# Input operators of an S5 mixer built with channel and position on the partitions: transposes in the mixer against more work in the preparation

## The chip, the cores and the metric

The kernel runs on one core of a Trainium2 chip. The core has a matrix engine (TensorE, PE in the profile; its weight loads are PEld), a vector engine (VectorE, DVE), a scalar engine (ScalarE, ACT), a general engine (GpSimd, POOL) and a sync engine (SyncE, SP), which here issues nearly all DMAs. Each engine works off its own queue in order. The metric is the device time of one execution in microseconds; lower is better.

## What is computed

The reference is a trunk of two layers over 512 positions of 1024 channels. Each layer is a half-step feed-forward block (FFN), a token mixer and a second FFN; layer 0 mixes by pooling, layer 1 by a bidirectional S5 state space. Only the S5 input side matters here:

```python
def s5_mixer(h, lam_re, lam_im, log_dt, b_re, b_im, c_re, c_im, d_skip, w_glu, b_glu):
    u = hf.reshape(Bsz, S, SSM_GROUPS, SSM_GROUP_DIM)          # 64 groups of 16 channels
    for direction in range(N_DIRS):
        ar, ai, bb_re, bb_im = zoh_discretise(lam_re[direction], ..., b_im[direction])
        bu_re = jnp.einsum('bsgh,gph->bsgp', u, bb_re)         # 64 states per group
        bu_im = jnp.einsum('bsgh,gph->bsgp', u, bb_im)
        xr, xi = complex_linear_scan(ar, ai, bu_re, bu_im, reverse=(direction == 1))
        y = y + einsum(xr, c_re) - einsum(xi, c_im)
    ...
```

## The kernel before

**Chunks.** The S5 mixer cuts the 512 positions into 64 chunks of L = 8. For a group, one matrix takes the 8 x 16 = 128 inputs of a chunk (position j, channel h) to the 64 complex states at the chunk's end. This matrix is a power of the transition times B, so its entries are products of a table over (state, j) and the given B over (state, h). There are 64 groups, two directions, real and imaginary part. They are called w1 here; w2 (states to outputs), w3 (inputs to outputs within a chunk) and rt (rotations for the scan) are its companions. All are made on the chip beforehand, written to DRAM (w1d, w2d, w3d, rd) and loaded again in the mixer, one batch b of eight groups at a time.

**Three stages of preparation** run in the background of the FFNs, as Python generators in a queue, `bgq`. Each call of `self.prep()` (L476) runs one to its next `yield`. `S5Prep.tables` (L132) makes the powers `pw` and the input table `gp` on DVE, in the first FFN of layer 0. `S5Prep.blocks` (L272) multiplies tables with B and C on POOL, in the second FFN of layer 0: 32 steps, one for each half batch hb and direction d. `products` (L283) makes E (for w2), bt and F (for w1) in ten POOL instructions, all from the helper `mul` (L277). `matrices` (L317) does 16 small matmuls (L326) on bt and E of both directions, evacuates them on ACT and DVE into kt, and stores E, F and kt. `S5Prep.rotation` (L212) makes rt on DVE in the first FFN of layer 1.

**Where the calls lie.** In an FFN, PE does 48 matmuls for each tile m of the hidden layer (two weights q) and calls `prep` after the first 24; in the output phase it is called after every second d. Weights come as `raw` by SP, are split by ACT and DVE into `whi`, `wlo` (L651, L652; `W.adv` prepares one and issues one DMA), and three matmuls (L658 to L660) stand for one product. Whatever is left in `bgq` is drained at hooks in the last output phase of an FFN: `spare` in layer 0, `operators` in layer 1.

**The transposes.** F lies with state on the partitions and (h, j) along the free axis. The mixer needs (j, h) on the partitions. `s5_flip` (L1093) therefore turns the loaded w1 of a batch on PE: 16 transposes of 128x128 (L1099) into four PSUM banks, and four ACT copies (L1100) back into w1. It is called eight times: w1[0] in a hook of the FFN before the mixer (L1638), w1[1] at its start, the others one or two batches ahead of use.

**The mixer's loop** (L1334). For a batch, `s5_state` (L1108) does 64 matmuls (L1119), then a chain on DVE: turn by rt (L1128), scan (L1141), turn back into X (L1128, L1150). `s5_out` does 16 matmuls with w3 (L1179) and 128 with X (L1187), ACT copies yj (L1192), `s5_turn` does 32 small ones (L1202). `s5_norm` (L1285, L1287, L1290) prepares the inputs u. From b = 2, `glu_mm` adds six matmuls of the gated layer behind the mixer.

## Time and profile before

| | |
|---|---|
| median of 3 runs (lowest to highest) | 1744.36 us (1743.97 to 1745.93) |
| the profiled execution's own time | 1743.41 us |
| its span, first to last instruction | 1741.5 us |
| mean granted TensorE clock | 0.984 of full |
| share of the span of DVE and POOL on the chain that ended last | 6% and 5% (PE 80%) |
| DMA packets | 126821, 290.62 MB |

The span is what the trace shows; 1.9 us of the execution lie around it. An engine's busy share says how much it works, not what the end waits for: for that one reads who made PE wait, and where. Matmuls are pipelined, so that one record (0.39 us for 512 columns) is longer than the distance to the next (0.23 us); costs on PE are taken from starts.

### The profile page before, as it was taken

Reading aid. Unit: us, or ns where it says so; the run is one execution under the profiler, and the core shown is the slowest. Engines: PE = TensorE matmul, PEld = TensorE weight load, DVE = VectorE, ACT = ScalarE, POOL = GpSimd, SP = SyncE. Lnnn points to the kernel's source line nnn. Section 1 sums busy time; section 2 is a strip of 40 time slices with the busy share of each in tenths; the row PEclk is TensorE's granted clock in tenths of the full one; section 3 lists DMA queues with packets and bytes.
Section 4 is the critical chain, followed back from the end, with each engine's and each line's share of the span. In section 5 each row is a group of like instructions: output and inputs, shape, how many; then the busy total and the mean of one; then the engine's idle time right before and its main releaser. Section 6 shows DMA issues by size and latency. Waiting matters only on the chain.

```text
span 1741.5 us, 25135 instructions
## 1 busy us (share of the span) xinstructions
PE 1686.2 (97%) x9872; PEld 1408.9 (81%) x9872; DVE 1135.3 (65%) x1845; ACT 573.8 (33%) x875; POOL 406.5 (23%) x370
## 2 busy tenths in 40 slices
PE   8999999998999999998999999987999999999997
PEld 6887888888887887887888888877888988888886
DVE  7768878678777667666766567647868654333435
ACT  5321322354321322233332233245633532222322
POOL 0000000056699999993000000001000000000000
PEclk9999999998999999998999999999999999999999
DMA  9357567441568777664443454487645253223321
GB/s 381 126 163 263 174 195 242 131 142 31 169 199 272 211 211 257 190 190 130 136 138 106 133 155 157 144 272 250 232 169 197 96 169 109 97 92 100 109 77 58
DMA packets 126821, 290.62 MB, mean 167 GB/s; under 512 B 19904, under 2 KB 57152, under 8 KB 125680
## 3 DMA queue, kind: packets, MB, share of 16 engines
q1 hardware_dynamic: 126080, 288.31, 51.0%
q8 instruction: 77, 1.26, 0.3%
q10 hardware_dynamic: 544, 0.52, 0.1%
q0 software_dynamic: 80, 0.20, 0.1%
q14 instruction: 40, 0.33, 0.1%
HBM read 261.85 MB, written 31.33 MB: 168 GB/s over the span
## 4 chain that ended last, share of the span: by engine, by line
PE 80%; DVE 6%; POOL 5%; DMA 4%; issue 2%; ACT 1%; SPq 1%; DVEq 0%; POOLq 0%; ACTq 0%
PE ps L658 24%; PE ps L659 24%; PE ps L660 24%; POOL e L277 3%; PE ps L605 2%; PE ps L1187 2%; DMA mw<-modw 2%; POOL E L277 1%; DVE tmp L713 1%; DMA raw<-win 1%; POOL F L277 1%; DVE hlo L716 1%; DVE mw L609 1%; POOL bt L277 1%; DVE wlo L652 1%
## 5 line engine op out<-in xcount | busy, mean ns | idle before, releaser
L658 PE MATMUL ps<-hlo,whi 128*128 128x512 f32 (+3 forms) x1488 | 566.0, 380 | 7.0 <-DVE hlo L716 6.9
L659 PE MATMUL ps<-hhi,whi 128*128 128x512 f32 (+3 forms) x1488 | 562.0, 378 | 0.0
L660 PE MATMUL ps<-hhi,wlo 128*128 128x512 f32 (+3 forms) x1488 | 561.6, 377 | 0.3 <-DVE wlo L652 0.3
L652 DVE TENSOR_TENSOR wlo<-raw,whi 128x1024 fp32r<-128x1024 f32 (+2 forms) x260 | 335.7, 1293 | 111.1 <-ACT whi L651 106.8
L651 ACT CAST whi<-raw 128x1024 fp32r<-128x1024 f32 (+2 forms) x273 | 274.2, 1010 | 374.4 <-PE ps L659 196.3
L658 PEld LDWEIGHTS ps<-hlo,whi 128*128 128x128 f32 x1488 | 280.8, 189 | 62.7 <-DVE hlo L716 6.5
L660 PEld LDWEIGHTS ps<-hhi,wlo 128*128 128x128 f32 x1488 | 281.1, 189 | 52.6 <-DVE wlo L652 0.8
L659 PEld LDWEIGHTS ps<-hhi,whi 128*128 128x128 f32 x1488 | 281.2, 189 | 50.5
L658 PE MATMUL ps<-glo,whi 128*128 128x512 f32 (+1 forms) x738 | 278.6, 378 | 0.0
L659 PE MATMUL ps<-ghi,whi 128*128 128x512 f32 (+1 forms) x738 | 278.0, 377 | 0.0
L660 PE MATMUL ps<-ghi,wlo 128*128 128x512 f32 (+1 forms) x738 | 278.0, 377 | 0.0
L609 DVE SCALAR_TENSOR_TENSOR mw<-mw,condb 128x1024 f32<-128x1024 f32 x144 | 198.5, 1385 | 21.2 <-DMA mw<-modw 20.8
L651 ACT CAST ghi<-tmp 128x512 fp32r<-128x512 f32 x96 | 59.6, 620 | 401.5 <-DVE tmp L727 395.4
L727 DVE TENSOR_TENSOR tmp<-ps,tmp 128x512 f32<-128x512 f32 x88 | 60.7, 690 | 171.0 <-PE ps L660 150.4
L658 PEld LDWEIGHTS ps<-glo,whi 128*128 128x128 f32 x738 | 140.3, 190 | 28.4 <-issue 0.6
L660 PEld LDWEIGHTS ps<-ghi,wlo 128*128 128x128 f32 x738 | 139.9, 190 | 27.7
L659 PEld LDWEIGHTS ps<-ghi,whi 128*128 128x128 f32 x738 | 140.0, 190 | 27.3
L732 DVE SCALAR_TENSOR_TENSOR x<-ps,m,x 128x512 f32<-128x512 f32 (+1 forms) x107 | 74.2, 694 | 111.2 <-PE ps L660 111.2
L652 DVE TENSOR_TENSOR glo<-tmp,ghi 128x512 fp32r<-128x512 f32 x96 | 74.8, 780 | 60.5 <-ACT ghi L651 60.4
L277 POOL TENSOR_TENSOR e<-T,pr 128x576 f32<-128x576 f32 x64 | 104.8, 1657 | 21.6 <-DMA pr<-s5bc 19.7
L970 POOL TENSOR_SCALAR x<-x,pbs 128x512 f32<-128x512 f32 (+1 forms) x10 | 15.3, 1535 | 362.4 <-ACT tmp L676 361.7
L1468 POOL TENSOR_TENSOR hhi<-hlo,rstd 128x256 f32<-128x256 f32 x3 | 2.7, 911 | 371.5 <-DVE rstd L697 371.5
(285 smaller groups left out, 1597.5 us busy)
## 6 DMA issues: line engine op xcount, KB each, us to landing
raw<-win SPq DMA_DIRECT2D x162, 512.0 KB, 3.6
mw<-modw SPq DMA_DIRECT2D x144, 512.0 KB, 4.7
raw<-wout SPq DMA_DIRECT2D x32, 512.0 KB, 3.6
raw<-wout SPq DMA_DIRECT2D x32, 448.0 KB, 3.3
raw<-wout SPq DMA_DIRECT2D x32, 384.0 KB, 3.1
w2d<-E SPq DMA_DIRECT2D x64, 128.0 KB, 4.6
w1d<-F SPq DMA_DIRECT2D x32, 256.0 KB, 4.2
w<-w1d SPq DMA_DIRECT2D x8, 1024.0 KB, 8.0
```

The costliest lines, as they stand in the source:

```text
L277: nc.gpsimd.tensor_tensor(out=o, in0=x, in1=y, op=op)
L605: nc.tensor.matmul(ps[m][q], lhsT=lhs[:, k], rhs=rhs, start=i == 3 * KD, stop=i == 1)
L609: self.nc.vector.scalar_tensor_tensor(out=w, in0=w, scalar=1.0, in1=self.condb, op0=ALU.mult, op1=ALU.mult, accum_out=dst)
L651: self.nc.scalar.copy(out=hi, in_=src)
L652: (eng or self.nc.vector).tensor_tensor(out=lo, in0=src, in1=hi.bitcast(F32), op=ALU.subtract)
L658: mm(ps, lhsT=hi[:, k], rhs=rhs[1][:, cs], start=start, stop=False)
L659: mm(ps, lhsT=hi[:, k], rhs=rhs[0][:, cs], start=False, stop=False)
L660: mm(ps, lhsT=lo[:, k], rhs=rhs[0][:, cs], start=False, stop=stop)
L713: nc.vector.scalar_tensor_tensor(out=t, in0=self.x[d][:, cs], scalar=A[:, d:d + 1], in1=r, op0=ALU.mult, op1=ALU.mult)
L727: nc.vector.tensor_tensor(out=t[0:n, cs], in0=pu[:, cs], in1=t[0:n, cs], op=ALU.mult)
L732: self.nc.vector.scalar_tensor_tensor(out=self.x[d][:, cs], in0=ps[:, cs], scalar=scale[:, d:d + 1], in1=self.x[d][:, cs], op0=ALU.mult, o ...
L1187: nc.tensor.matmul(o(HB * h + g + e), lhsT=X[d][k][r, ri, g + e], rhs=w2[r, d, g + e, ri ^ k], start=False, stop=d + k + ri + g // 2 == 4)
```

## The change

w1 is now made directly with (channel h, position j) on the 128 partitions, as [part, group, state] along the free axis. `tables` turns `gp` on PE (eight matmuls against a 64x64 identity for each direction), copies it on ACT into `tu`, and writes it with 16 small DMAs to a DRAM table `ud`; the DVE copies U1 and U2 are gone. In `blocks`, `params` issues two more DMAs for each step, each spreading 2 KB rows over partitions (`ud` over the 16 channels, the given B, as a new input `s5bt`, over the 8 positions; 256 KB each). F is made from these: two products of 128x512, then a difference and a sum of 128x256 each, in place of two products and one sum of 128x512. `s5_flip` and its eight calls go.

The order changes too. E and F of a step are stored two steps later (`store`), `matrices` of hb runs a step later (bt has 4 buffers), a last step stores the rest, and an FFN's tail calls `prep` once more if it is the layer's second. In layer 1 `early` loads w1, w2 and w3 of batch 0 ahead of the rotation instead of behind it.

```diff
@@ tables
+            ps = psum.tile([P, 8, 64], F32, name="ps")
+            for ri in range(2):
+                for kb in range(4):
+                    nc.tensor.matmul(ps[:, 4 * ri + (kb if d else 3 - kb)], lhsT=gp[0:64, ri, 2 * kb:2 * kb + 2],
+                                     rhs=ident[0:64, 0:64], start=True, stop=True)
+            tu = pool.tile([P, 2, 4, 64], F32, name="tu")
+            nc.scalar.copy(out=tu.rearrange("p r k n -> p (r k) n"), in_=ps)
+            for k2 in range(2):
+                for ri in range(2):
+                    for k in range(4):
+                        nc.sync.dma_start(out=self.ud[d, 2 * k + (k2 if d else 1 - k2), :, ri],
+                                          in_=tu[64 * k2:64 * k2 + 64, ri, k])
+            yield
-            v.tensor_copy(out=o(self.U1), in_=gp[:, 0, js])
-            v.tensor_scalar(out=o(self.U2), in0=gp[:, 1, js], scalar1=self.sgn, scalar2=-1.0,
-                            op0=ALU.mult, op1=ALU.mult)
@@ blocks: params
+            ub = pool.tile([P, 2, 2, HB * 64], F32, name="ub", bufs=2)
+            for i, t in enumerate((self.ud[d, :, hb].rearrange("j r g n -> j (r g n)").unsqueeze(0),
+                                   I["s5bt"][d, hb].unsqueeze(1))):
+                nc.sync.dma_start(out=ub[:, i].rearrange("p r x -> p (r x)"),
+                                  in_=t.to_broadcast([16, L, 2 * HB * 64]))
@@ blocks: products
-            sf = [P, HB, 16, 8]
+            sf = [P, 2, HB * 64]
-            ub = lambda t: t[:, d, gs].unsqueeze(2).to_broadcast(sf)
-            bb = lambda k: pr[:, k].unsqueeze(3).to_broadcast(sf)
-            mul(f1, ub(self.U1), bb(2))
-            mul(f2, ub(self.U2), bb(3))
-            mul(Ft, f1, f2, ALU.add)
+            mul(f1, ub[:, 0, 0:1].to_broadcast(sf), ub[:, 1])
+            mul(f2, ub[:, 0, 1:2].to_broadcast(sf), ub[:, 1])
+            mul(Ft[:, 0], f1[:, 0], f2[:, 1], ALU.subtract)
+            mul(Ft[:, 1], f1[:, 1], f2[:, 0], ALU.add)
@@ blocks: the loop
-            if before:
-                matrices(*before)
-            made = [products(hb, 0)]
-            yield
-            shifts()
-            made.append(products(hb, 1))
-            before = hb, made
-            yield
+            made = []
+            for d in range(2):
+                if len(stores) > 1:
+                    store(*stores.pop(0))
+                if d and before:
+                    matrices(*before)
+                made.append(products(hb, d))
+                stores.append((hb, d, *made[d][1:]))
+                if d:
+                    before = hb, made
+                yield
+                if d == 0:
+                    shifts()
+        for o in stores:
+            store(*o)
+        yield
@@ ffn, tail
+                if f:
+                    self.prep()
@@ s5_state
-                                         lhsT=w1[:, 2 * h + d, g, 64 * ri:64 * ri + 64], rhs=ut[:, h * HB + g],
+                                         lhsT=w1[:, 2 * h + d, ri, g], rhs=ut[:, h * HB + g],
@@ s5_mixer, three calls, and one in the FFN before it
-        self.s5_flip(w1[1])
-            self.s5_flip(w1[b + 2])
-                    self.s5_flip(w1[b + 4])
-                                before=[operators, lambda: self.s5_flip(ops0[0][0])] + [
-                                    load(i) for i in (2, 3)])
+                                before=[operators, lambda: None] + [load(i) for i in (2, 3)])
@@ early
+                    for i in (0, 1, 3):
+                        ops0[i][0] = loads[i](pre, 0)
+                        yield
                     yield from self.prep3()
-                    for i, f in enumerate(loads):
-                        yield
-                        ops0[i][0] = f(pre, 0)
+                    yield
+                    ops0[2][0] = loads[2](pre, 0)
```

## Rows read from the trace of the kernel before

**Rows 1.** Busy time, share of the span and instructions of each engine, from the page.

```profile
PE 1686.2 (97%) x9872; PEld 1408.9 (81%) x9872; DVE 1135.3 (65%) x1845; ACT 573.8 (33%) x875; POOL 406.5 (23%) x370
```

**Rows 2.** What PE waited for, whole span: line waited for, us in total, times, longest.

```profile
PE ps L326 <- POOL bt L277: 10.0, 3, 5.8
...
PE ps L1099 <- DMA w<-w1d: 5.1, 1, 5.1
```

**Rows 3.** PE in order of time around the first turn of w1: start us, us, line, operation, count, and in brackets the idle time before it with what ended it.

```profile
1138.69 0.39 PE L841 MATMUL ps<-ghi,tws 128*128 128x512 f32 x1
...
1143.44 0.56 PE L1227 MATMUL ps<-m,ident 128*16 128x8 f32 x16
1149.13 3.67 PE L1099 MATMUL ps<-ident,w 128*128 128x128 f32 x16 [5.13 <-DMA w<-w1d]
1152.46 0.78 PE L841 MATMUL ps<-ghi,tws 128*128 128x512 f32 x1
```

**Rows 4.** PE in order of time in the mixer.

```profile
1186.99 3.34 PE L1099 MATMUL ps<-ident,w 128*128 128x128 f32 x16
...
1217.25 1.98 PE L1179 MATMUL ps<-w,hhi 128*64 128x128 f32 x16 [6.26 <-ACT yj L1192]
...
1226.86 1.97 PE L1099 MATMUL ps<-ident,w 128*128 128x128 f32 x16
...
1279.05 0.50 PE L658 MATMUL ps<-hlo,whi 128*128 128x512 f32 x1
...
1288.50 3.72 PE L1187 MATMUL ps<-w,X 64*64 64x128 f32 x128
```

**Rows 5.** DVE in order of time in the mixer; L1287 ends the inputs of batch 0, each L1128 with tmp<-ps,rt starts the chain of a batch (b = 0, 3, 6, 7 here), the last L1150 ends that of batch 7.

```profile
1188.97 0.69 DVE L1287 TENSOR_TENSOR hhi<-hhi,shift 128x512 f32<-128x512 f32 x1
...
1191.68 1.89 DVE L1128 TENSOR_TENSOR tmp<-ps,rt 128x512 f32<-128x512 f32 x3 [0.69 <-PE ps L1119]
1193.48 3.68 DVE L1128 TENSOR_TENSOR z<-tmp 128x256 f32<-128x256 f32 x2
...
1219.93 1.24 DVE L1141 TENSOR_TENSOR_SCAN ws<-d,z 128x519 f32<-128x519 f32 x1 [2.32 <-ACT d L1125]
...
1228.26 0.69 DVE L652 TENSOR_TENSOR hlo<-tmp,hhi 128x512 fp32r<-128x512 f32 x1 [2.28 <-ACT hhi L651]
...
1229.47 1.88 DVE L1128 TENSOR_TENSOR tmp<-ps,rt 128x512 f32<-128x512 f32 x3
...
1263.17 1.88 DVE L1128 TENSOR_TENSOR tmp<-ps,rt 128x512 f32<-128x512 f32 x3
...
1272.79 1.88 DVE L1128 TENSOR_TENSOR tmp<-ps,rt 128x512 f32<-128x512 f32 x3
...
1281.47 0.42 DVE L1150 SCALAR_TENSOR_TENSOR X<-ws,rt 128x256 f32<-128x256 f32 x1
```

**Rows 6.** Busy time (and instructions) of PE, PEld, DVE, ACT and POOL in the stretch in which `blocks` runs evenly, then granted clock, DMA share and GB/s.

```profile
452.50:680.00 227.50, 223.32 (x1096) 178.93 (x1097) 164.63 (x161) 60.04 (x89) 220.59 (x198) 1.00 0.74 230
```

**Rows 7.** Line 277, all POOL instructions of `products`: count, duration in ns as min/median/max, first and last start.

```profile
L277 POOL TENSOR_TENSOR e<-U,pr x64: 1062/1072/2055, 425.1 to 792.4; 128x512 f32<-128x512 f32 x64
L277 POOL TENSOR_TENSOR E<-e,e x32: 1422/1442/2300, 422.3 to 787.8; 128x576 f32<-128x576 f32 x32
...
L277 POOL TENSOR_TENSOR bt<-bt,b x32: 319/324/1199, 424.8 to 791.1; 128x64 f32<-128x64 f32 x32
L277 POOL TENSOR_TENSOR F<-e,e x32: 1282/1486/2242, 427.5 to 793.6; 128x512 f32<-128x512 f32 x32
```

**Rows 8.** POOL on line 652, both inputs full: count, min/median/max ns.

```profile
L652 POOL TENSOR_TENSOR wlo<-raw,whi x13: 1845/2395/2647, 372.3 to 1360.0; 128x1024 fp32r<-128x1024 f32 x12, 128x768 fp32r<-128x768 f32 x1
```

**Rows 9.** Groups of POOL instructions: busy us, mean ns | idle before us, releaser.

```profile
L277 POOL TENSOR_TENSOR e<-T,pr 128x576 f32<-128x576 f32 x64 | 104.8, 1657 | 21.6 <-DMA pr<-s5bc 19.7
L277 POOL TENSOR_TENSOR e<-U,pr 128x512 f32<-128x512 f32 x64 | 82.4, 1307 | 0.0
...
L277 POOL TENSOR_TENSOR F<-e,e 128x512 f32<-128x512 f32 x32 | 51.8, 1618 | 2.5
```

**Rows 10.** DVE and POOL in order of time, one meeting of the two.

```profile
496.10 2.31 DVE L609 SCALAR_TENSOR_TENSOR mw<-mw,condb 128x1024 f32<-128x1024 f32 x1
...
497.40 3.16 POOL L277 TENSOR_TENSOR e<-T,pr 128x576 f32<-128x576 f32 x2
```

**Rows 11.** POOL at the start of steps 3 and 32 of `blocks`, and PE at its small matmuls, in order of time.

```profile
452.46 2.76 POOL L277 TENSOR_TENSOR e<-T,pr 128x576 f32<-128x576 f32 x2 [14.23 <-DMA pr<-s5bc]
...
679.96 0.44 PE L326 MATMUL ps<-E,bt 128*32 128x128 f32 x4 [3.90 <-POOL bt L277]
...
784.87 2.88 POOL L277 TENSOR_TENSOR e<-T,pr 128x576 f32<-128x576 f32 x2
785.24 0.42 PE L326 MATMUL ps<-E,bt 128*32 128x128 f32 x8
...
791.49 0.66 PE L326 MATMUL ps<-E,bt 128*32 128x128 f32 x8 [5.83 <-POOL bt L277]
```

**Rows 12.** PE at the start of tile m = 8 of the first FFN, and DVE in `tables`, direction 0: the last instruction on the table gp (in the step of m = 11), and the first of the step after it (m = 12), in order of time.

```profile
157.06 0.39 PE L658 MATMUL ps<-hlo,whi 128*128 128x512 f32 x1
...
201.97 0.69 DVE L130 TENSOR_TENSOR gp<-ct,cu 128x512 f32<-128x512 f32 x1
...
208.33 1.28 DVE L202 TENSOR_SCALAR T<-pw,sgn 128x576 f32<-128x576 f32 x1
```

More of the change, by code (lines that the diff above doesn't have):

```diff
@@ L80, in alloc_keep @@
         self.T2 = keep.tile([P, 2, NG, 9], F32, name="T2")
-        self.U1 = keep.tile([P, 2, NG, 8], F32, name="U1")
-        self.U2 = keep.tile([P, 2, NG, 8], F32, name="U2")
         self.f1 = keep.tile([P, 2, NG], F32, name="f1")
@@ L130, in cmul, with tables @@
             v.tensor_tensor(out=o, in0=t, in1=u, op=op)
-    def tables(self, pool):
+    def tables(self, pool, psum, ident):
         nc, I = self.nc, self.I
@@ L197, in tables @@
             yield
+            ps = psum.tile([P, 8, 64], F32, name="ps")
[11 more added lines that the diff above has]
+            yield
             ks = slice(None) if d == 0 else slice(None, None, -1)
-            js = slice(None, None, -1) if d == 0 else slice(None)
             o = lambda t: t[:, d].rearrange("p g k -> p k g")
@@ L333, in matrices @@
             nc.vector.tensor_tensor(out=kt[:, 7], in0=kv[1][:, 7], in1=kt[:, 7], op=ALU.add)
-            for d, (_, E, Ft) in enumerate(parts):
-                ws = slice(1, 9) if d == 0 else slice(0, 8)
-                for ri in range(2):
-                    nc.sync.dma_start(out=self.w2d[b, hh, :, d, :, ri].rearrange("p g (k h) -> p g k h", h=16),
-                                      in_=E[64 * ri:64 * ri + 64, :, ws])
-                nc.sync.dma_start(out=self.w1d[b, 2 * hh + d], in_=Ft.rearrange("p g h j -> p (g h j)"))
             nc.sync.dma_start(out=self.kbd[gs].rearrange("q h k -> (q h) k"), in_=kt.rearrange("p k h -> p (k h)"))
@@ L342, in matrices, with store @@
                 self.late = b
+        def store(hb, d, E, Ft):
+            b, hh = divmod(hb, GB // HB)
+            ws = slice(1, 9) if d == 0 else slice(0, 8)
+            for ri in range(2):
+                nc.sync.dma_start(out=self.w2d[b, hh, :, d, :, ri].rearrange("p g (k h) -> p g k h", h=16),
+                                  in_=E[64 * ri:64 * ri + 64, :, ws])
+            nc.sync.dma_start(out=self.w1d[b, 2 * hh + d], in_=Ft.rearrange("p r n -> p (r n)"))
         def shifts():
@@ L355, in blocks @@
         before = self.late = None
+        stores = []
         self.pr = {}
@@ L1091, in s5_spare @@
         self.W.issue()
-    def s5_flip(self, w1):
-        nc = self.nc
-        for i in range(4):
-            ps = self.psum.tile([P, HB, P], F32, name="ps")
-            for g in range(HB):
-                nc.tensor.transpose(ps[:, g], w1[:, i, g], self.ident)
-            nc.scalar.copy(out=w1[:, i], in_=ps)
     def s5_rt(self, pool, b):
@@ L1483, in prep1 @@
         with tc.tile_pool(name="tab", bufs=1) as p:
-            yield from S.tables(p)
+            yield from S.tables(p, self.psum, self.ident)
     def prep3(self):
@@ L1724, in host_arrays @@
     k = np.stack([np.concatenate(t, 0) for t in ((cr, ci), (ci, cr), (br, bi), (bi, br))], 0)
+    bt = np.stack([A(t)[0] for t in (ssm_b_re, ssm_b_im)], 0)
+    a["s5bt"] = bt.reshape(2, 2, NG // HB, HB, 64, 16).transpose(1, 2, 5, 0, 3, 4).reshape(2, NG // HB, 16, 2 * HB * 64)
     a["s5bc"] = k.reshape(4, P, 2, NG // HB, HB, 16).transpose(1, 2, 3, 0, 4, 5)
```

19 lines of the change are left out of this document (10 added, 9 removed).

## Prediction

> **What bounds the kernel now.** I read the busy shares first. PE works 97% of the span [rows 1], so time comes back in two ways only: PE gets less to do, or one of its few waits goes. Second, the list of PE's waits. Two of them touch this change: 10.0 us on POOL's bt, in front of the small matmuls of `matrices`, and 5.1 us on the load of w1[0] [rows 2]. Third, the order of time on PE around the transposes [rows 3, 4], and on DVE in the mixer [rows 5], because there PE is not always the bound. Fourth, POOL in the preparation: between 452.5 and 680 it is busy for 220.6 of 227.5 us [rows 6]. So `blocks` runs at POOL's pace, and it ends the stage: PE stands 5.8 us at the last small matmuls until step 32 has made its bt [rows 11]. The change takes work from PE in the mixer and gives POOL more in the stage where POOL is full. The sum is the difference of two costs of like size.
>
> **The first turn of w1.** PE is free at 1144.0 (1143.44 and 0.56), waits for the load of w1[0], turns it in 3.67 us and starts the next product at 1152.46 [rows 3]. Without transposes that product starts at 1144.0, and the load comes 30 steps of background work earlier. Gain 8.5 us. What could stand in its place: `early` now runs the rotation three steps later, so some 18 DVE instructions of about 0.4 us, 7.8 us in all (an estimate from the 0.69 us of a 512-element product [rows 12], scaled to 256 elements), fall into the hook `operators` together with the stores of rd and the load of rt[0]. Three prepared weights, each 20 matmuls or 4.7 us on PE (1138.69 to 1143.44 [rows 3]), cover that; if they did not, a few us of the 8.5 are lost.
>
> **The other seven turns.** Two bounds. Upwards: the turns' own PE time, 3.34 us for w1[1] and 1.97 for each of six [rows 4], 15.2, and the 6.26 us for which `s5_out` of batch 1 waits on yj [rows 4]; the four PSUM banks of a turn are what fills the eight there, so that wait should go. Together 21. Downwards: what the DVE chain gives back. The u of batch 0 is ready at 1189.7 while the first chain starts at 1191.68 [rows 5], so the turn of w1[1] hides behind the norm. From there DVE works without a break but for 2.32 us on ACT's d0 copies [rows 5], which wait behind `s5_norm`, not behind the turns; that wait stays. A chain without a norm takes 9.62 us when nothing holds it (batch 6 to 7), one with a norm 0.69 more, 10.3 [rows 5]. Ahead of batch 3 DVE stands 2.28 us for ACT [rows 5], which goes, as ACT no longer copies w1 and PE no longer waits at 1217; then batch 3 starts at 1227.2 for 1229.47, batch 6 (10.3, 10.3 and 9.7 later) at 1257.5 and batch 7 at 1267.1 against 1272.79: 5.7 us. After the chains PE is the bound: before, X[7] is there at 1281.9 and PE takes it at 1288.50 only [rows 4, 5], as it is late by its turns. After, PE ends batch 6 at about 1268.5, does the turn of y (1.0), 36 product matmuls (8.4, 1279.05 to the L1179 before 1288.50) and 1.0 of L1179, and takes X[7] at 1278.9. Gain 9.6. I take 8.5: GpSimd's split of two weights, which costs DVE 2.9 us at 1193.48 (3.68 us for two instructions of 256 elements, where one of 512 takes 0.69 [rows 5]), starts some 3 us earlier without ACT's copies and then meets the norm of batch 0.
>
> **The added work in `tables`.** 16 matmuls with 128 stationary columns; the nearest row is the turn, 1.97 us for 16 [rows 4]. They wait for gp, ready at 202.66; PE reaches them one step later, at m = 12 after 24 matmuls: 216 matmuls of 0.227 us behind 157.06, so 206 [rows 12]. No wait. Cost 1.9 us. Two ACT copies of 0.6 us lie beside PE; four DVE copies go. The 32 SP stores stand in front of weight loads for some 7 us each time, and the three or four prepared weights of 5.4 us cover that. Direction 1's last DVE step slips into the hook `mixer`, under five output products of PE.
>
> **`blocks`: the step on POOL.** This is the term that decides. Uncontended, an instruction of 512 elements with an inner broadcast takes 1.062 us (e<-U,pr), one with two full inputs 1.282 (F), of 64 elements 0.319 [rows 7]. From F and bt<-bt,b: 0.18 us fixed and 2.15 ns per element; 1024 full elements then make 2.38, and the row says 2.395 [rows 8]. In the new step neither input of f1 and f2 is broadcast along the inner axis (only over re and im, outside 256 elements), so they cost 1.282 each, and the two halves 0.73 each. New 4.03, old 2 x 1.062 + 1.282 = 3.41: **0.62 us more a step**. Bounds: f1 and f2 as cheap as before, 0.18 more (one more instruction); or contention grows with the instructions. Means stand above minima by 0.245 (e<-U,pr) and 0.336 (F) [rows 7, 9]; with 0.336 on each of the four, 5.38 against 2 x 1.307 + 1.618 = 4.23, 1.15 more.
>
> I take no growth: what POOL loses is lost to single DVE instructions. At 497.40 two products that need 2.32 take 3.16, right behind DVE's mw, which itself stretches to 2.31 [rows 10]; DVE's number of those is set by PE's pace, not by POOL's. The Trainium skill (SBUF — State Buffer, "Who interferes with whom") says that a DVE instruction with two SBUF inputs contends with a GpSimd instruction that reads SBUF. By that rule the trace agrees: mw and e<-T,pr wait in turn [rows 10], and the sum is the one with 0.62; without the rule it would be the one with 1.15.
>
> **`blocks`: the end.** From step 3 (452.46) POOL goes on until the bt of step 32 releases PE at 791.49 [rows 11]. 29 of these steps grow by 0.62: 18.0 us. Against that, POOL stood idle for 21.6 us before its steps, 14.2 of them ahead of step 3 [rows 9, 11]; those 14.2 stay (nothing that the diff moves lies ahead of that load on SP), of the other 7.4 I take 5 as given back, as SP no longer stands at E and F ahead of the loads and as POOL will be late anyway. So bt of step 32 comes 13.0 us later, and PE waits for it: the last `matrices` still follow the last step directly. Later `matrices` and the extra call in the tail only move PE's other waits (3.90 us at 679.96 [rows 11]) into this last one. What a slower clock behind those waits costs is hidden in it too. Cost 13.0; ends 0.2 (0.18 a step) and 28 (1.15 a step).
>
> **`blocks`: DMAs.** 64 loads of 256 KB are 16.8 MB over 340 us, 49 GB/s on top of 230 at a DMA share of 0.74 [rows 6]: about 0.90, still below full. Stores keep their number. SP stands at a store or at ub's buffer only when POOL is late, and then PE stands too. I take 0; if weights came late it would cost some us.
>
> **Sum.** -8.5 - 8.5 + 1.9 + 13.0 = -2.1 on the profiled execution's own 1743.41: 1741.3. The median of the runs is 0.95 above that execution, so 1742.
>
> **The rivals.**
> *Cheap products.* If f1 and f2 cost what the U products did, the step grows by 0.18 and POOL ends 0.2 later: -8.5 - 8.5 + 1.9 + 0.2 = -14.9, 1728.5 (runs 1729). For it: they are multiplications as those were, and the full rows are sums and differences. Against: nothing else in the rows explains 1.062 beside 1.282 but the broadcast. The Trainium skill (GPSIMD Engine Reference, "3.1 Elementwise — side-by-side cycle accounting") gives about 2.6 cycles per element for any two-input instruction, without a word on broadcasts, and so speaks for this rival; the two rows differ by 20%, and the measurement decides.
> *POOL slows further, and the change is slower.* The mechanism is POOL's queue at the last `matrices`: every 0.1 us a step costs 2.9 us there. With 1.15 a step the cost is 28: +12.9, 1756.3 (runs 1757). It is slower than before beyond what can be measured from 0.83 a step on. For it: means well above minima [rows 7, 9]. Against: the meeting in rows 10.
> *The mixer gives back less.* DVE binds to the end: of 8.5 only 5.7 less the 2.9 of the split's meeting, 2.8; +3.6, 1747. For it: DVE's unbroken run [rows 5]. Against: X[7] lies 6.6 us before PE takes it.
> *POOL's lateness hides.* If deferring covers it, the 10.0 us of waits go: -8.5 - 8.5 + 1.9 - 10.0 = -25.1, 1718. Against: the last products still precede the last matrices.
>
> **How the numbers follow.** Forecast 0.46, cheap products 0.17, slower POOL 0.18, less in the mixer 0.12, hidden 0.07. 0.2%, 3.5 us, is about what a measurement can tell from no change. The forecast spreads by some 5 us around -2.1: 0.18 faster, 0.24 same, 0.04 slower. With cheap products and the hidden case as faster, slower POOL as slower, and the mixer case 0.05 same and 0.07 slower: faster 0.42, same 0.29, slower 0.29. The range from 1728 to 1756 takes in all but the hidden case and the far end of the slow one. The likeliest case alone spans 1737 to 1747.
>
> **What would show it.** In the profile after: no L1099; PE going from L1227 to the next product without a gap, some 8.5 us saved; e products of 512 at a minimum of 1.28 and halves at 0.73; the wait for bt at the last small matmuls about 13 us longer in sum, and the first product behind it that much later; the mixer from the norm of batch 0 to X[7] on PE 8 to 10 us shorter, with DVE unbroken. I am wrong if POOL's minima stay at 1.06, if POOL is not full between the stage's ends, or if new waits for DMAs appear in front of weights.

## The result, and the profile after

The changed kernel takes 1758.24 us (median of four runs, 1757.59 to 1758.81) against 1744.16 for the kernel before; the ratio is 1.0081 with a 95% interval of 1.0063 to 1.0098. It is 14 us slower where 2 us faster was forecast, and 2 us outside the range. The profiled execution has a span of 1757.0 us, 15.5 more than before.

The busy shares (first part of the page) give no hint: PE has 4 us less to do than in [rows 1] and POOL 24 us more.

```profile
PE 1682.1 (96%) x9776; PEld 1404.4 (80%) x9776; DVE 1129.7 (64%) x1841; ACT 558.8 (32%) x845; POOL 430.1 (24%) x402
```

The list of what PE waited for (line waited for, us in total, times, longest) gives the first one. Of the waits in [rows 2] the one on w1 is gone and the one on bt has grown from 10.0 to 24.5 us. A wait of 4.6 us on DVE's inputs of batch 0 is new.

```profile
PE ps L341 <- POOL bt L286: 24.5, 5, 10.4
...
PE ps L1138 <- DVE hhi L1306: 4.6, 1, 4.6
```

A list of waits does not say where time is lost for good. For that the same instruction is looked up on PE in both traces, and the difference of the starts is followed from stage to stage:

| instruction on PE | before | after | later by |
|---|---|---|---|
| first product behind direction 1's matmuls of `tables` | 348.48 | 352.79 | 4.3 |
| first product of the second FFN of layer 0 | 411.79 | 419.92 | 8.1 |
| last small matmuls of `blocks` | 791.49 | 818.01 | 26.5 |
| first output product of the last part, layer 1 | 1134.04 | 1161.63 | 27.6 |
| second output product | 1138.69 | 1167.42 | 28.7 |
| third, behind where w1[0] was turned | 1152.46 | 1172.65 | 20.2 |
| last sum before the mixer | 1185.21 | 1210.07 | 24.9 |
| X of batch 7 taken | 1288.50 | 1304.68 | 16.2 |
| end of the span | 1741.5 | 1757.0 | 15.5 |

The two falls are the gains: 8.5 at the first turn and 8.7 in the mixer, against forecasts of 8.5 and 8.5. The four rises are the costs: 8.1 up to the second FFN (forecast 1.9), 18.4 in `blocks` (13.0), 1.1 behind it, and 5.8 around rotation's end (0).

Around the former turn, PE in order of time (start us, us, line, operation, count; lines of products left out): the answer to [rows 3] is that the product at 1172.65 follows the small matmuls of 1172.17 at once.

```profile
1167.42 0.40 PE L869 MATMUL ps<-ghi,tws 128*128 128x512 f32 x1
...
1172.17 0.56 PE L1246 MATMUL ps<-m,ident 128*16 128x8 f32 x16
1172.65 0.50 PE L869 MATMUL ps<-ghi,tws 128*128 128x512 f32 x1
```

The products of `blocks` on POOL (duration in ns as min/median/max, first and last start), the answer to [rows 7]:

```profile
L286 POOL TENSOR_TENSOR e<-T,pr x64: 1156/1172/2157, 427.9 to 814.3; 128x576 f32<-128x576 f32 x64
L286 POOL TENSOR_TENSOR e<-ub x64: 1269/1298/2289, 433.3 to 819.1; 128x512 f32<-128x512 f32 x64
L286 POOL TENSOR_TENSOR F<-e,e x64: 727/1592/1720, 436.1 to 821.2; 128x256 f32<-128x256 f32 x64
```

The minima, 1.269 and 0.727 us, are close to what was forecast (1.282 and 0.73), so the "cheap products" are out. The median of the halves is twice their minimum: most of them wait, as POOL and DVE do in [rows 10]. The trace shows for what. From step 3 to step 32, 9 of the 58 halves have no DVE instruction with two inputs in SBUF (neither of them in PSUM, where PE's results lie) beside them, and these take 0.73 to 0.74 us; the other 49 take 1.45 us in the mean. From step 3 to step 32, busy time of PE, PEld, DVE, ACT and POOL, granted clock, DMA share and GB/s, first before, then after:

```profile
452.46:784.87 332.41, 328.23 (x1599) 263.34 (x1596) 233.90 (x228) 91.35 (x138) 318.32 (x290) 0.99 0.71 219
```

```profile
462.70:813.21 350.51, 330.81 (x1617) 264.10 (x1615) 232.28 (x229) 92.98 (x140) 341.42 (x319) 0.97 0.80 251
```

POOL's idle time falls from 14.1 to 9.1 us, the 5 us that the prediction gave back. Its busy time rises by 23.1 us, 0.80 a step and not 0.62. Its step 32 starts at 813.21, and PE stands at the last small matmuls until that step has made its bt (in [rows 11] 784.87 and 791.49); POOL, then PE:

```profile
813.21 2.28 POOL L286 TENSOR_TENSOR e<-T,pr 128x576 f32<-128x576 f32 x2
```

```profile
818.01 0.65 PE L341 MATMUL ps<-E,bt 128*32 128x128 f32 x8 [10.36 <-POOL bt L286]
```

ACT waits longer than before for weights of the FFNs' output phases, and what is added all lies in this stage (whole span, before, then after). PE's own list has no wait for a DMA, so this did not reach PE.

```profile
ACT whi L651 <- DMA raw<-wout: 6.8, 1, 6.8
```

```profile
ACT whi L677 <- DMA raw<-wout: 36.2, 10, 11.8
```

In `tables`, eight matmuls take 2.00 us each time (each makes two records), and behind those of direction 1 SP is held for 10 us by 16 stores, ahead of the weights of the pooling stage. PE, then SP's queue:

```profile
206.93 2.00 PE L201 MATMUL ps<-ident,gp 64*128 64x64 f32 x16
350.87 2.00 PE L201 MATMUL ps<-ident,gp 64*128 64x64 f32 x16
```

```profile
353.51 10.08 SPq L208 DMA_DIRECT2D ud<-tu  x16
363.69 0.53 SPq L419 DMA_DIRECT2D raw<-band  x1
```

Around rotation's end, DVE in order of time. In the kernel before it stands 9.6 us for the store of rd, three steps earlier:

```profile
1094.21 0.19 DVE L258 COPY R<-th 128x16 f32<-128x16 f32 x1 [9.60 <-DMA rd<-R]
```

In the changed kernel it stands 7.7 us for it just ahead of the last two `gate_up`s (tmp), which are late; 18 products drained by `operators` follow from 1168.29 on, ahead of the next x.

```profile
1154.41 0.18 DVE L267 COPY R<-th 128x16 f32<-128x16 f32 x1 [7.71 <-DMA rd<-R]
...
1160.57 0.69 DVE L753 TENSOR_TENSOR tmp<-ps,tmp 128x512 f32<-128x512 f32 x1
...
1164.50 0.68 DVE L753 TENSOR_TENSOR tmp<-ps,tmp 128x512 f32<-128x512 f32 x1
...
1168.29 0.42 DVE L127 TENSOR_TENSOR ct<-R,W 128x256 f32<-128x256 f32 x1
```

PE's waits from there to the mixer:

```profile
1166.62 0.50 PE L684 MATMUL ps<-glo,whi 128*128 128x512 f32 x1 [0.87 <-DVE glo L678]
...
1194.09 0.39 PE L686 MATMUL ps<-ghi,wlo 128*128 128x256 f32 x1 [1.40 <-POOL wlo L678]
...
1200.19 2.30 PE L1284 MATMUL ps<-acc,hhi 128*128 128x32 f32 x16 [1.55 <-DVE acc L1281]
```

At the start of the mixer GpSimd's two splits (1213.63, 5.14 us together) now lie on the norm of batch 0, and DVE's 0.69 us become 2.72 and 2.85. From 1219.96 on DVE has work without a break but for the one wait of 2.32 us on ACT, as forecast. DVE:

```profile
1213.10 0.69 DVE L1304 TENSOR_TENSOR hhi<-hhi,r 128x512 f32<-128x512 f32 x1
1213.82 2.72 DVE L1306 TENSOR_TENSOR hhi<-hhi,shift 128x512 f32<-128x512 f32 x1
1216.47 2.85 DVE L1304 TENSOR_TENSOR hhi<-hhi,r 128x512 f32<-128x512 f32 x1
1219.35 0.69 DVE L1306 TENSOR_TENSOR hhi<-hhi,shift 128x512 f32<-128x512 f32 x1
1219.96 1.88 DVE L1147 TENSOR_TENSOR tmp<-ps,rt 128x512 f32<-128x512 f32 x3
```

### The profile page after: what moved, and what is told of

The parts are those of the page before. It is cut to its first block, busy times and chain, and to the rows that moved or that the text cites. A ratio compares the mean times of both kernels' runs of the same rounds, so it can differ in the third digit from the quotient of the medians.

```text
span 1757.0 us, 25105 instructions
## 1 busy us (share of the span) xinstructions
PE 1682.1 (96%) x9776; PEld 1404.4 (80%) x9776; DVE 1129.7 (64%) x1841; ACT 558.8 (32%) x845; POOL 430.1 (24%) x402
## 4 chain that ended last, share of the span: by engine, by line
PE 76%; DVE 9%; DMA 7%; POOL 3%; issue 2%; ACT 2%; SPq 1%; DVEq 0%; ACTq 0%; POOLq 0%
PE ps L684 23%; PE ps L686 23%; PE ps L685 23%; PE ps L631 2%; DMA mw<-modw 2%; POOL e L286 2%; DVE mw L635 1%; DMA raw<-win 1%; DMA ubuf<-hlo 1%; DVE tmp L739 1%; DVE hlo L742 1%; DVE wlo L678 1%; PE ps L1206 1%; DVE ws L1160 1%; DMA w1d<-F 1%
## 5 line engine op out<-in xcount | busy, mean ns | idle before, releaser
L635 DVE SCALAR_TENSOR_TENSOR mw<-mw,condb 128x1024 f32<-128x1024 f32 x144 | 194.7, 1360 | 27.4 <-DMA mw<-modw 27.0
L286 POOL TENSOR_TENSOR e<-ub 128x512 f32<-128x512 f32 x64 | 101.7, 1609 | 0.0
```

Of the source, the lines that this page charges most:

```text
L286: nc.gpsimd.tensor_tensor(out=o, in0=x, in1=y, op=op)
L635: self.nc.vector.scalar_tensor_tensor(out=w, in0=w, scalar=1.0, in1=self.condb, op0=ALU.mult, op1=ALU.mult, accum_out=dst)
```

## The experiments

Ratios are to the kernel before; the changed kernel has 1.0081. A thousandth is 1.7 us.

**The gain alone.** The kernel before, `s5_flip` emptied.

```diff
     def s5_flip(self, w1):
-        nc = self.nc
-        for i in range(4):
-            ps = self.psum.tile([P, HB, P], F32, name="ps")
-            for g in range(HB):
-                nc.tensor.transpose(ps[:, g], w1[:, i, g], self.ident)
-            nc.scalar.copy(out=w1[:, i], in_=ps)
+        pass
```

> The kernel before, with the body of s5_flip left out: w1 is used as loaded, so the input operators are wrong and the work of the transposes and of ACT's copies is missing; all else is as before, blocks and rotation included. Theory (both mixer terms of the prediction were right): the first turn gives 8.5 us and the other seven 8.5, so about 1727 (ratio 0.990). Rival (the mixer is bound by DVE's chain and gives the turns' time back there): 8.5 and at most 3, so 1733 or more. Of the 17 some may be seen more here than in the changed kernel, as GpSimd's two weight splits at the start of the mixer then come at another time.

1725.65 us, ratio 0.9906 (0.9891 to 0.9921): 16.4 us, interval 13.8 to 19.0. Both mixer terms hold together, and the meeting of GpSimd's splits with the norm is there as well (PE waits 4.58 us at 1183.53). The loss of the changed kernel lies outside the mixer: some 30 us.

**POOL's step made short.** The changed kernel with one product for F.

```diff
-            f1 = pool.tile(sf, F32, name="e1")
-            f2 = pool.tile(sf, F32, name="e2")
...
-            mul(f1, ub[:, 0, 0:1].to_broadcast(sf), ub[:, 1])
-            mul(f2, ub[:, 0, 1:2].to_broadcast(sf), ub[:, 1])
-            mul(Ft[:, 0], f1[:, 0], f2[:, 1], ALU.subtract)
-            mul(Ft[:, 1], f1[:, 1], f2[:, 0], ALU.add)
+            mul(Ft, ub[:, 0, 0:1].to_broadcast(sf), ub[:, 1])
```

> The changed kernel, with F made by one product of 512 elements: the second product, the difference and the sum are left out, so F is wrong. Theory (POOL's pace ends the stage of blocks): the step on POOL falls by 1.28 and two times 0.73, 2.7 us, below PE's pace; the waits of PE for bt, 24.5 us in the changed kernel, go nearly all, and the time falls by 20 to 27 us to 1731 to 1738. Rival (the stage is late for another reason: the 64 added loads and their 256 KB each, or SP's queue): the waits for bt change their name to a DMA or to weights, and the time falls by less than 10 us, to 1748 or more.

1728.13 us, 0.9915 (0.9900 to 0.9931), 29 us below the changed kernel and so a little more than expected. No wait on bt is left, and the last small matmuls start at 783.14 instead of 818.01, without a wait. The 64 added loads are still there; no wait of PE on a DMA is. POOL's step is the cause in `blocks`, not the traffic.

**The price of a microsecond on POOL.** The kernel before, with one needless product of 256 elements in each step.

```diff
             mul(Ft, f1, f2, ALU.add)
+            flat = lambda t: t.rearrange("p g h j -> p (g h j)")[:, 0:256]
+            mul(flat(f1), flat(f2), flat(Ft))
```

> The kernel before, with one product of 256 elements more in each step on POOL, written over a tile that is no longer needed; the outputs stay as they are, POOL's step grows by 0.73 us, and nothing else of the change is there. It measures what a microsecond on POOL's step costs at the end. Theory (POOL ends blocks; 29 steps of 0.73 are 21 us, and of POOL's idle time ahead of its steps at most 2 us come back): 19 to 23 us more than before, 1763 to 1767. Rival (the prediction's 5 us of idle time come back, so 16 us): 1758 to 1761. A second rival (the changed kernel's loss in blocks came from the added loads and their traffic, not from POOL's step): less than 10 us.

1764.10 us, 1.0113 (1.0100 to 1.0127): 20 us. From step 3 to 32, POOL's busy time is 343.64 of 355.02 us: 25.3 more than before, 0.87 for a product of 0.73, and 11.4 us idle instead of 14.1. So this added instruction, too, costs more than its own time, here 0.14 a step. The theory's number holds, though under it lie 25.3 us of busy time and not 21, and 2.7 us of idle time that came back. From step 3 to 32, busy time of PE, PEld, DVE, ACT and POOL, granted clock, DMA share and GB/s:

```profile
455.31:810.33 355.02, 331.79 (x1601) 263.62 (x1599) 231.85 (x229) 92.98 (x139) 343.64 (x320) 0.98 0.66 206
```

**The order of `blocks`.** The changed kernel with matrices and stores where they were.

```diff
-                if d and before:
-                    matrices(*before)
...
+            if before:
+                matrices(*before)
+            made = [products(hb, 0)]
```

> The changed kernel, with the order of blocks as in the kernel before: matrices at the start of a half batch, E and F stored there, no extra call in the tail. Theory (later matrices only move PE's waits into the last one, as POOL ends the stage): the waits for bt come back in earlier places but the last small matmuls end within 3 us of the changed kernel, and the time is 1755 to 1761. Rival (deferring is what hides POOL's lateness): the sum of the waits grows by 10 us or more and the time with it. A second rival (deferring costs: POOL waits for the E and F buffers that are stored two steps later): the time falls by more than 4 us.

1756.12 us, 1.0064 (1.0048 to 1.0080). The last small matmuls start at 819.98 instead of 818.01; the waits on bt are 22.2 us in eight places. While POOL ends the stage, the order moves waits and neither hides nor costs what these runs can tell.

**bt on DVE.** The changed kernel; POOL's step loses 1.1 us.

```diff
-            nc.gpsimd.memset(bt[:, :, 16:32], 0.0)
-            mul(bt[:, :, 0:16], fb(self.f1), pr[:, 2])
-            mul(b2, fb(self.f2), pr[:, 3])
-            mul(bt[:, :, 0:16], bt[:, :, 0:16], b2, ALU.add)
+            def small():
+                tt = nc.vector.tensor_tensor
+                nc.vector.memset(bt[:, :, 16:32], 0.0)
+                tt(out=bt[:, :, 0:16], in0=fb(self.f1), in1=pr[:, 2], op=ALU.mult)
+                tt(out=b2, in0=fb(self.f2), in1=pr[:, 3], op=ALU.mult)
+                tt(out=bt[:, :, 0:16], in0=bt[:, :, 0:16], in1=b2, op=ALU.add)
+            self.small.append(small)
```

`small` is called at the start of the next step, ahead of `params`.

> The changed kernel, with the four small instructions that make bt moved from POOL to DVE, one step later (bt of a step is made when the next step is issued). POOL's step loses 3 x 0.32 and a memset of 0.15: 12.09 - 1.1 = 11.0 us, less than the 11.46 of the kernel before. Theory (POOL's pace ends blocks): POOL no longer falls behind, nearly all of the 24.5 us of waits go as they did with one product, minus what DVE loses by four small instructions a step (three of them may each stand behind one POOL instruction of about 1.3 us): the time falls by 18 to 28 us, to 1730 to 1740. Rival (POOL and DVE share one path to memory, so that the work only changes its engine): DVE's products of weights come late instead, PE gets new waits on wlo or glo of more than 10 us, and the time falls by less than 10 us.

1739.23 us, 0.9972 (0.9961 to 0.9984): 19 us below the changed kernel, and faster than the kernel before. PE's waits on bt, now made by DVE:

```profile
PE ps L348 <- DVE bt L325: 4.4, 2, 3.9
```

The 3.9 us are at the last small matmuls (800.91). A wait of 4.1 us on glo is new.

**The same in the kernel before**, first one step later by the same edit (`small` is called ahead of `matrices`, too), then in the same step:

```diff
-            nc.gpsimd.memset(bt[:, :, 16:32], 0.0)
-            mul(bt[:, :, 0:16], fb(self.f1), pr[:, 2])
...
+            en = nc.vector if hb > 1 else nc.gpsimd
+            en.memset(bt[:, :, 16:32], 0.0)
+            en.tensor_tensor(out=bt[:, :, 0:16], in0=fb(self.f1), in1=pr[:, 2], op=ALU.mult)
...
```

The first of the two:

> The kernel before, with bt made on DVE one step later (that of the last step at once); the transposes in the mixer and everything else stay. POOL's step falls by 1.1 to about 10.4. Theory (POOL's lateness cost the kernel before only the 10.0 us of waits that its trace shows, and DVE takes a few us back): 1735 to 1739. The changed kernel with the same move has 1739, so with POOL out of the way the change as it was made would be worth about nothing: 17 gained in the mixer, 8 lost ahead of blocks, 5 by rotation, some more by POOL and DVE. Rival (moving bt relieves the contention of POOL and DVE as well, as with one product): 1728 to 1733, and the changed kernel would lose even so.

1811.33 us, 1.0394 (1.0372 to 1.0415), which neither theory had. pr has two buffers, and read one step later a buffer comes free one step later; its load then stands behind stores on SP. POOL's waits:

```profile
POOL e L277 <- DMA pr<-s5bc: 151.0, 29, 17.8
```

So it does not tell what bt on DVE is worth. The second run does:

> The kernel before, with bt made on DVE in the same step (from hb = 2 on; POOL makes it before that), so that pr is read no later than before and its buffer comes free no later; the transposes and everything else stay. It repeats the question of the run with bt one step later, where POOL waited 151 us for pr and so did not show what was asked. POOL's step is about 10.4, below PE's pace. Theory (POOL's lateness cost the kernel before only the 10.0 us of waits of its trace, DVE takes a few back): 1735 to 1741, about what the changed kernel with bt on DVE has (1739), so that the change as it was made is worth nothing even with POOL out of the way, because of its losses in tables, the pooling stage and rotation. Rival (DVE waits for pr in its turn and hands the wait on to PE): 1745 or more, with new waits of DVE on DMA pr.

1741.73 us, 0.9993 (0.9983 to 1.0003): no gain that these runs can tell, and just above the range that was expected. A single wait on bt is left, at the very last small matmuls:

```profile
PE ps L327 <- DVE bt L306: 7.7, 1, 7.7
```

POOL itself stands 0.88 us for pr ahead of step 32 here, and PE waits at the end all the same. So of the 10.0 us in [rows 2], the 5.8 at the end need not be backlog of POOL: the last `matrices` follow the last products directly, and PE waits for the step to run through. With matrices a step later and a POOL that keeps up, no wait is left at this place in the run with one product and in the version with all edits (below), and 3.9 us in the run with bt on DVE. With bt on DVE in both, the change is worth 0.0021 (0.000 to 0.004 by the two intervals), about 4 us, not 17; the two runs make bt at different places in the step, so this is not the change alone.

**Rotation first.** The changed kernel with `early` in its old order.

```diff
-                    for i in (0, 1, 3):
-                        ops0[i][0] = loads[i](pre, 0)
-                        yield
                     yield from self.prep3()
-                    yield
-                    ops0[2][0] = loads[2](pre, 0)
+                    for i, f in enumerate(loads):
+                        yield
+                        ops0[i][0] = f(pre, 0)
```

> The changed kernel, with the order of early put back: rotation first, then the loads of w1, w2, rt and w3 of batch 0. Theory (the 4.7 us that the end of this FFN gives back come from rotation's last DVE instructions and the wait of 7.7 us on the stores of rd, which fall into the last output phase): rd is stored 3 steps earlier, DVE's wait on rd goes, the weights behind it are prepared in time, and the time falls by some 5 us to 1753. Rival (the loss comes from GpSimd's lazy splits and the slower clock there, whatever the order): within 2 us of the changed kernel. A second rival: w1 of batch 0 comes late again, and PE waits up to 5 us for it in front of the first matmuls of s5_state rather than for the turn.

1754.17 us, 1.0064 (1.0047 to 1.0081), 3 to 4 us less. The interval overlaps that of the changed kernel, so the gain rests on the trace. There the way from the end of `blocks` (sum product after the spare weights) to the first matmuls of `s5_state` is 378.25 us (834.55 to 1212.80) instead of 383.62 (832.98 to 1216.60): 5.4. DVE still waits for the store of rd, 8.5 us at the longest, but in an earlier step; PE's waits on wlo (1.4 us) and on acc ahead of the last sums (1.55) are gone, and none on w1 has come.

**Four stores in place of 16.** The table ud in DRAM gets another layout, so that one DMA takes four positions; the two products of F read it through other views, with the same minimum of 1.27 us.

```diff
-                for ri in range(2):
-                    for k in range(4):
-                        nc.sync.dma_start(out=self.ud[d, 2 * k + (k2 if d else 1 - k2), :, ri],
-                                          in_=tu[64 * k2:64 * k2 + 64, ri, k])
+                for ri in range(2):
+                    nc.sync.dma_start(out=self.ud[d, (k2 if d else 1 - k2)::2, :, ri].rearrange("j g n -> g j n"),
+                                      in_=tu[64 * k2:64 * k2 + 64, ri])
...
```

> The changed kernel, with ud written by 4 DMAs for each direction in place of 16 (the table in DRAM holds re and im side by side for each group; the operands of the two F products follow in that order). Theory (SP was held 10 us by 16 stores ahead of the weights of the pooling stage, which made its weights and its first x late): SP is held some 3 us, the pooling stage of layer 0 starts as much later as tables costs alone (about 4.4 us instead of 8.1), and the time falls by 3 to 4 us. Rival (direction 1's last DVE step, which now falls into the drain at the start of the mixer of layer 0, is what makes DVE late there): no change there, within 1 us. Where POOL ends blocks, some of the gain may be lost behind it: POOL's step 3 then starts earlier by the same amount.

```profile
352.99 2.56 SPq L207 DMA_DIRECT2D ud<-tu  x4
356.88 0.33 SPq L422 DMA_DIRECT2D raw<-band  x1
```

SP is held 2.56 us instead of 10.08, and the second FFN of layer 0 starts at 415.67: 3.9 us later than before instead of 8.1. The theory is right about the place. DVE's step of direction 1 still falls into the hook, so that rival falls. But the time is 1756.63 us with the same ratio, 1.0081 (1.0066 to 1.0096), where 3 to 4 us less were expected; the two intervals together leave room for a gain of that size. In the traces the gain is 6.0 us at the last small matmuls (812.03), 4.6 at the last sums, 3.0 at the start of the mixer and 1.8 at the end of the span. The last section says what took 1.6 of it.

**Transposes in `tables`.**

```diff
-                    nc.tensor.matmul(ps[:, 4 * ri + (kb if d else 3 - kb)], lhsT=gp[0:64, ri, 2 * kb:2 * kb + 2],
-                                     rhs=ident[0:64, 0:64], start=True, stop=True)
+                    nc.tensor.transpose(ps[:, 4 * ri + (kb if d else 3 - kb)],
+                                        gp[0:64, ri, 2 * kb:2 * kb + 2].rearrange("p a b -> p (a b)"), ident[0:64, 0:64])
```

> The changed kernel, with the 16 matmuls of gp against an identity in tables made as transposes. Theory (the term was mis-sized because a matmul with full-precision operands costs more than one of the transposes that it was sized by: 0.25 us against 0.123): 8 of them take 1.0 us or less in place of 2.00 each time, and the first product behind them comes 2 us earlier in sum; the end of the run gains 0 to 2 us, as much as blocks and DMA let through. Rival (the 0.25 us are the weight loads of 64 x 128 columns, which transposes need as well): still 2.0 us each time, no change.

```profile
207.29 0.71 PE L201 MATMUL ps<-ident,gp 64*128 64x64 f32 x8
349.94 0.71 PE L201 MATMUL ps<-ident,gp 64*128 64x64 f32 x8
```

0.089 us each instead of 0.25; 2.6 us are saved in sum. The last small matmuls start 2.5 us earlier (815.55), and again the end of the span is where it was (1757.0 us; the time is 1758.69 us, ratio 1.0069, 1.0048 to 1.0090).

**The splits at the mixer's start on DVE,** behind the norms.

```diff
-        W.prep(nc.gpsimd)
-        W.prep(nc.gpsimd)
...
         u = [self.s5_norm(ut[b], b) for b in range(2)]
+        W.prep()
+        W.prep()
```

> The changed kernel, with the two weight splits that GpSimd does at the start of the S5 mixer given to DVE, behind the norms of batches 0 and 1, where DVE waits for PE's 128 small matmuls. Theory (GpSimd's two splits of 5.1 us stretch DVE's norm of batch 0 from two times 0.7 to 2.7 and 2.85 us, and PE waits 4.57 us for it): that wait shrinks by about 4 us, the first chain on DVE starts as much earlier, and as the chains are unbroken the time falls by 3 to 4.5 us to about 1754. Rival (DVE's chain is the bound of the mixer and now holds two splits of 1.0 more): the gain is at most 2 us.

```profile
1210.41 0.19 DVE L1291 SCALAR_TENSOR_TENSOR rstd<-ps,rstd 128x32 f32<-128x32 f32 x1 [3.60 <-ACT rstd L1290]
...
1211.59 0.69 DVE L1306 TENSOR_TENSOR hhi<-hhi,shift 128x512 f32<-128x512 f32 x1
1212.20 0.68 DVE L1304 TENSOR_TENSOR hhi<-hhi,r 128x512 f32<-128x512 f32 x1
...
1213.53 2.35 DVE L678 TENSOR_TENSOR wlo<-raw,whi 128x1024 fp32r<-128x1024 f32 x2
1215.80 1.88 DVE L1147 TENSOR_TENSOR tmp<-ps,rt 128x512 f32<-128x512 f32 x3
```

1755.39 us, 1.0057 (1.0041 to 1.0073), 3 to 4 us less. Without GpSimd beside them the norm's instructions take 0.69 us each, and PE's wait is 2.5 us instead of 4.6. From rstd to the first chain DVE needs 5.4 us instead of 7.3. Of the expected 4 us, 1.9 show there; the rest of the timed gain is within the interval.

**All of it.** bt on DVE (in the last step at once), rotation first, four stores, transposes, splits on DVE.

> The changed kernel with five edits together: bt on DVE one step later (that of the last step at once), rotation ahead of the loads in early, four stores of ud for each direction, transposes in tables, and the two splits at the start of the mixer on DVE. Theory (the changed kernel lost in blocks, tables, the pooling stage and rotation what it gained in the mixer, and these losses are separate): 1739 with bt on DVE alone, less 4 (rotation), less 2 to 4 (stores), less 0 to 2 (transposes), less 2.5 (splits), so 1727 to 1731, faster than both kernels (ratio to before about 0.991). Rival (the end is held by one bound, DVE, once POOL no longer ends blocks, and the gains do not add): 1735 to 1740.

1729.41 us, 0.9917 (0.9902 to 0.9932): 14.5 us faster than the kernel before, 28.6 than the changed one, and within the range that was expected for losses that are separate and add. The single gains were 19 (bt), 3 to 4 (rotation), 0 to 2 (stores), 0 to 2 (transposes) and 3 to 4 (splits); making the last bt at once, which the run with bt on DVE did not, is part of the sum. What is late next stands behind `blocks`:

```profile
PE ps L722 <- DVE acc L716: 9.0, 1, 9.0
```

```profile
805.95 1.99 ACT L689 CAST whi<-raw 128x1024 fp32r<-128x1024 f32 x2 [8.19 <-DMA kbd<-kt]
```

The hook `spare` splits two weights into memory that `blocks` gives up. ACT waits there for the last store of kt, and DVE's x and acc stand behind the splits. In the changed kernel PE's wait at this place is 2.7 us.

**bt's products on ACT** in that version.

```diff
+                        nc.scalar.activation(out=bt[:, q, 16 * h:16 * h + 16], in_=pr[:, k, q], func=AF.Identity,
+                                             scale=t[:, d, g:g + 1])
...
+                nc.vector.tensor_tensor(out=bt[:, :, 0:16], in0=bt[:, :, 0:16], in1=bt[:, :, 16:32], op=ALU.add)
```

The products of a step are made in the next one, their sum one step later still, in front of `matrices`.

> As the version with all five edits, with the two products of bt on ACT (eight small instructions for a step, scaled by a column) and only the sum and the fill with zeros on DVE. Theory (in that stage DVE is nearly full where POOL's and DVE's instructions meet, ACT is busy for a quarter of the time): DVE is relieved of two products of about 0.5 us a step, PE's waits on glo and on bt fall by some us, and the time is 1 to 5 us below the version with DVE alone. Rival (ACT's small instructions stand in front of the weights' casts, eight times about 0.2 us, and the weights come later): same or up to 5 us more.

```profile
PE ps L360 <- DVE bt L329: 30.6, 13, 5.2
```

1754.08 us, 1.0050 (1.0032 to 1.0068), 25 us more than with DVE alone, five times what the rival allowed, and for another reason. The sum falls into the same step as the matmuls that read it, and stands behind DVE's other work of that step, mostly an mw, at some places an x for which DVE waits on PE. So PE waits up to 5.2 us, 2.4 in the mean, at 13 of 16 `matrices`.

## Why the prediction was wrong, step by step

- **The first turn of w1**, 8.5: right, 8.5. Its cover was not: see rotation.
- **The other seven turns**, 8.5 between bounds of 5.7 and 9.6: right, 8.7, and 16.4 (13.8 to 19.0) for both in the run without turns. The reason for the value taken, the split's meeting with the norm, was seen: 2.72 and 2.85 us.
- **`tables`**, "Cost 1.9 us" by the nearest row, a turn of 0.123 us: failed, 4.3. The row was a transpose and the added instruction a plain matmul, 0.25 us instead of 0.089 for a transpose of the same size; the run with transposes shows it. The Trainium skill (FP8 and Floating Point Precision, "TensorE Precision Notes") gives four passes through the array for true FP32. Here a matmul has two records and takes 2.8 times a transpose of the same size, so the trace shows neither four records nor four times the time, and the measurement decides.
- **The 32 SP stores**, "three or four prepared weights of 5.4 us cover that": failed, 3.8. Direction 1's stores come in the last output phase, where weights of 4.7 us alternate with the pooling stage's own loads, and hold SP for 10 us, not 7. The run with four stores shows place and cause.
- **The step on POOL**, "I take no growth": failed, in the stage that the prediction said decides. Uncontended, the step is 0.59 us longer by the minima of both traces, close to the 0.62 of the sum. Busy time grew by 0.80, so about 0.2 a step is contention, 5.1 us above the sum; the needless product shows 0.14. The text had 0.62 without growth and 1.15 with it, and the first was taken because PE's pace sets how many instructions DVE has. But what POOL issues beside them counts too: 49 of the 58 new halves lie beside one and take 1.45 us instead of 0.73. By the rule of the Trainium skill (SBUF — State Buffer, "Who interferes with whom") a DVE instruction with two SBUF inputs contends with a GpSimd instruction that reads SBUF. That the trace agrees (0.69 us with GpSimd away, 2.72 with it) says who waits, but not that POOL's share stays the same when POOL issues more.
- **The end of `blocks`**, 13.0: 18.4. The 5 us of idle time came back as forecast. 13.0 and 5.1 of contention and 2.1 that steps 1 and 2 lost, which "29 of these steps" left out, less 1.8 in the last step's own run (6.62 to 4.80 us), make the 18.4. Behind it another 1.1 are lost; the cause was not followed up.
- **Rotation three steps later**, "Three prepared weights ... cover that; if they did not, a few us of the 8.5 are lost": failed, 5.8. The weights covered the beginning (no gap at 1172.65), not the end: PE waits 0.9 us for glo, 1.4 for a wlo and 1.55 for acc, the last with a slower clock behind it. What was not looked for is DVE's own wait of 7.7 us for the store of rd, which moved with the 18 products to just ahead of the last two `gate_up`s.
- **DMAs of `blocks`**, 0: right for PE, which in this stage waits for bt and, as before, for DVE's and ACT's work, but for no DMA. One engine earlier weights did come late: ACT stood 36.2 us for them instead of 6.8.

In sum: -8.5 - 8.7 + 8.1 + 18.4 + 1.1 + 5.8 - 0.7 (rest) = 15.5. Against the forecast of -2.1 that is 17.6 us: 5.8 at rotation and 3.8 at the stores, both put at nothing, 5.4 in `blocks`, 2.4 for the matmuls of `tables`, 1.1 behind `blocks`, less 0.2 and 0.7. No single step made the miss.

The rival that came nearest, "POOL slows further", had the right mechanism for `blocks`. That its time agrees, 1757 to 1758, is luck: with the measured 0.80 a step instead of its 1.15, the prediction's own sum gives +3.1, or 1746.5, and the other losses made up the rest. (By that sum the change is slower beyond 3.5 us from 0.81 a step on, not 0.83.) Of the three signs of being wrong, two did not appear (the minimum of the e products is 1.27, and POOL is busy for 341.42 of 350.51 us), and the third, waits for DMAs in front of weights, appeared on ACT and did not reach PE. None of them watched the stores of `tables` or rotation, the two terms that were put at nothing.

## What to carry to other kernels

Before work is moved into a stage, ask which engine ends that stage: here 0.73 us more on each of POOL's steps came back as 20 us at the end, and moving 1.1 us of small instructions off POOL gave 19. Size an added instruction by a row of the same kind, not only of the same shape, and add contention when the engine that takes it is full (here 0.14 and 0.2 us a step, for 0.73 and 0.59 added). A moved step takes its own waits with it (a store that its buffer waits for, an operand's buffer that comes free later): 7.7 us of such a wait made late what the cover was counted for, and one of this kind cost 67 us.

## What the runs showed of the hardware

**The lower clock can eat a gain.** PE's wait of 1.55 us ahead of the last sums (1200.19 in the changed kernel) is followed by products of 256 columns 0.21 us apart, at the lower of the two clock levels, 1.2 GHz; then they stand 0.12 us apart, at 2.4 GHz. That slow stretch lasted 4.8 us in the changed kernel. With rotation first there is no such wait, and the products behind the sums stand 0.12 us apart at once. With four stores the same wait came 4.6 us earlier and the slow stretch behind it took 7.8 us. The way from these sums to the first matmuls of `s5_state` took 17.97 us instead of 16.41. In both traces (busy time of PE, PEld, DVE, ACT and POOL, granted clock, DMA share, GB/s):

```profile
1200.19:1216.60 16.41, 11.83 (x88) 11.72 (x89) 6.31 (x12) 7.27 (x15) 3.18 (x6) 0.75 0.93 272
```

```profile
1195.59:1213.56 17.97, 13.39 (x89) 13.27 (x89) 6.31 (x12) 7.22 (x15) 3.19 (x6) 0.72 0.90 273
```

What decides when the clock comes back, and where the last 1.2 us go in the mixer, stays open. Single gains of 2 to 3 us ahead of that place did not show in the time; in the version with all edits they are part of a sum that does.
